# A fourth feature block of the down projection in seven half products, the blocks spread over a pair of output columns, and the second gate's sums spread evenly over the gate and up stage

## The chip, the cores and the metric

The kernel runs on one core of one Trainium2 chip. The metric is the device time of one execution in microseconds (us); lower is better. The core has a matrix engine (TensorE, PE in the profile; its weight loads are PEld), a vector engine (VectorE, DVE), an activation engine (ScalarE, ACT), GpSimd (POOL) and a sync engine (SP), from whose queue nearly all transfers are issued.

## The reference, cut to what matters

The reference is one layer of a diffusion transformer over 256 latent tokens and 256 context tokens, in float32, with a model width of 2048 and a hidden width of 5632. After attention, its output projection and a layer norm comes the part that the change touches:

```python
def swiglu(u, w_gate, w_up, w_down):
    return (jax.nn.silu(u @ w_gate) * (u @ w_up)) @ w_down
...
sh1, sc1, g1, sh2, sc2, g2 = ada_mods(c, w_ada[layer], b_ada[layer])
...
x = layer_norm(DN_ALPHA * x + g2 * swiglu(modulate(x, sh2, sc2), w_gate[layer], w_up[layer], w_down[layer]),
               ln2_g[layer], ln2_b[layer])
```

Here `u` is 256 x 2048, `w_gate` and `w_up` are 2048 x 5632, `w_down` is 5632 x 2048. The vector `g2` is the "second gate": 2048 numbers, each the product of the 2048 entries of `silu(c)` with a column of `w_ada`.

## The kernel before, in words

**Products in three passes.** A float32 product is made of three matmuls. Each operand is split into a rounded part `hi` (a copy on ScalarE) and the rest `lo` (a subtraction on VectorE), and `mm3` (L280 to L283) issues hi x hi, hi x lo and lo x hi into one bank of PSUM. `load_split` loads a piece of weights of 512 x 512 (1024 KB) into one of four `raw` buffers and splits it in two operations per engine, of 128 x 1024 each (`split_raw`, L271 and L272; `split`, L277 and L278, does the same for other operands). There are four pairs of `hi` and `lo` buffers, so the splits can be two plain steps ahead of TensorE.

**Gate and up stage.** The hidden width is cut into 11 blocks of 512. For each block `f` a step `project` multiplies 512 of the 2048 model features with 512 columns of `w_gate` or `w_up`, for both halves of the tokens: 24 matmuls. Some of the first steps of each block were done earlier (their sums lie in `spills`). In the stage shown here, blocks 0 to 2 have 6 steps left, blocks 3 to 9 have 4, block 10 has 8: 54 in all. At a block's end `activate` makes silu(gate) * up on VectorE and ScalarE. Then `flip_steps` transposes the result: `squares` within 32 x 32 squares, `put` through DRAM and `get` back (eight stores and two loads on SP), and `place` splits it into `hTh[f]` and `hTl[f]`. These steps are due a fixed number of `turn()` calls later (`PUT`, `GET`, `PLACE`, `QUARTERS`); each step of the gate, up and down stages makes one call, and a block in half products two. Buffers are shared: `hTh[f]` takes the memory of the spill of block f-1.

**The second gate's sums.** `gate2_steps(i)` gives 14 steps for 1024 columns of the gate: eight that load 1024 KB of `w_ada` each and add them up on VectorE in two operations (`vector_sum`, L400), and six that sum over the partitions with TensorE. They use the same `raw` buffers as the weights. `merge` puts lists of steps together evenly. Before, the first half is merged with blocks 0 to 2 (18 steps), the second with blocks 7 to 10 (20 steps); blocks 3 to 6 run without sums, and at their first steps `residual_base` prepares the residual with rows of the layer norm (tile `lgb`, two loads and four VectorE operations per block).

**Down stage.** The output width is four column blocks of 512, handled as two pairs (`pair(0)`, `pair(2)`). A `plain` step multiplies one feature block by 512 columns, for both halves of the tokens: 24 matmuls, two splits on ScalarE and VectorE each. For the blocks in `QUARTERS` the product of a pair, with both operands in 2 x 2 parts (halves of tokens and of features; halves of features and the two column blocks), is made of seven products in place of eight (Winograd's form of Strassen's method): `by_quarters` issues 7 x 6 = 42 matmuls instead of 48. For it `quarter_sums` makes four sums s1 to s4 of parts of the activations once per block, and splits them; and VectorE makes four combinations of the parts of the weights for each pair, each 128 x 1024, between the seven splits. The banks named a and c gather the first column block for the two halves of the tokens, b and d the second, and p1, p5, p6 and p7 are added in at the end (`combine_parts`). `first_block` and `second_block` apply the gate and add the residual. After the last matmuls comes the second layer norm (`ending`).

The order of work is the program's order, in which the tile framework places each engine's instructions as their inputs and buffers come free; within the last lines (`manual_schedule`) it is as written. The order of the feature blocks is given by hand:

```python
QUARTERS = {8: (9, 13), 9: (10, 11), 10: (9, 9)}
ORDER = (0, 1, 8, 2, 3, 9, 4, 5, 6, 10, 7)
```

Each entry of `QUARTERS` holds the turns after which the block's placement and its sums are due. The first column block of a pair runs through all of `ORDER`, with blocks 8, 9 and 10 in half products for both column blocks at once; then the second column block runs through the eight plain blocks.

## Time and profile before

| | before |
|---|---|
| median of 3 runs | 1134.63 us (1134.55 to 1135.07) |
| the profiled execution | 1133.65 us, its span 1131.9 us |
| mean granted clock of TensorE | 0.995 |
| busy: TensorE, VectorE, ScalarE | 1105.7, 923.0, 588.6 us |
| first matmul of the down stage | at 886.42 us |
| start of the last matmul | at 1118.36 us |

A row of the profile's groups names the line and engine, the operation, output and inputs, shapes, the count, then the busy time and the mean duration of one in ns, and last the idle time of the engine before them with what ended it. A row of the timeline begins with start and duration in us. A row of the waits has what waited, what it waited for, and the total, the number and the longest.

### The profile page before, as it was taken

The numbers are of one execution on the slowest core, as the hardware profiler recorded it, in microseconds if no ns is written. First come the engines' busy times: TensorE is split into PE (matmuls) and PEld (weight loads), VectorE is DVE, ScalarE is ACT, GpSimd is POOL, SyncE is SP. The second block draws the span as 40 slices with busy tenths as digits, with TensorE's granted clock in tenths as the row PEclk, the third lists the DMA queues.
The fourth block names the chain that finished last, engine by engine and source line by source line (L and its number), as shares of the span: only waits on it lengthen the run. The fifth ranks groups of instructions, "written<-read, shape, count | busy, mean of one in ns | idle before, by whom it ended". The sixth has DMA issues, their size and how long they took to land. (4 is left out here: it accounts for less than half of the span.)

```text
span 1131.9 us, 14173 instructions
## 1 busy us (share of the span) xinstructions
PE 1105.7 (98%) x5241; PEld 894.3 (79%) x5241; DVE 923.0 (82%) x1133; ACT 588.6 (52%) x843; POOL 41.5 (4%) x79
## 2 busy tenths in 40 slices
PE   8999999999999999999999999999989999999995
PEld 6766778777888788888888888888778888888884
DVE  3768999999998997877699767879874899678876
ACT  3444584977784365444564544454344565345541
POOL 1000050101200010000000000000000000000000
PEclk9999999999999999999999999999999999999998
DMA  9999999687999789989889877779887576546651
GB/s 293 383 384 397 381 354 362 229 302 224 354 339 384 277 295 347 347 285 350 276 275 336 314 233 254 238 245 317 305 302 260 153 253 223 190 148 228 225 216 74
DMA packets 179241, 321.26 MB, mean 284 GB/s; under 512 B 8762, under 2 KB 51162, under 8 KB 176867
## 3 DMA queue, kind: packets, MB, share of 16 engines
q1 hardware_dynamic: 177364, 319.25, 81.2%
q10 hardware_dynamic: 1808, 1.11, 0.4%
q8 instruction: 41, 0.67, 0.2%
q14 instruction: 28, 0.23, 0.1%
HBM read 304.07 MB, written 16.25 MB: 283 GB/s over the span
## 5 line engine op out<-in xcount | busy, mean ns | idle before, releaser
L272 DVE TENSOR_TENSOR lo<-raw,hi 128x1024 fp32r<-128x1024 f32 x234 | 282.0, 1220 | 115.2 <-ACT hi L271 107.5
L271 ACT CAST hi<-raw 128x1024 fp32r<-128x1024 f32 x234 | 244.7, 1054 | 239.9 <-PE acc L283 206.5
L282 PE MATMUL acc<-lo,u2h 128*128 128x512 f32 x704 | 275.2, 391 | 3.1 <-DVE lo L272 3.1
L281 PE MATMUL acc<-hi,u2h 128*128 128x512 f32 x704 | 274.2, 391 | 2.4 <-ACT hi L271 2.4
L283 PE MATMUL acc<-hi,u2l 128*128 128x512 f32 x704 | 275.0, 391 | 1.2 <-DVE u2l L1630 1.2
L282 PEld LDWEIGHTS acc<-lo,u2h 128*128 128x128 f32 x704 | 132.5, 188 | 31.9 <-DVE lo L272 4.6
L281 PEld LDWEIGHTS acc<-hi,u2h 128*128 128x128 f32 x704 | 132.5, 188 | 31.1 <-ACT hi L271 2.8
L283 PEld LDWEIGHTS acc<-hi,u2l 128*128 128x128 f32 x704 | 132.5, 188 | 29.7 <-DVE u2l L1630 2.1
L549 ACT CAST hi<-raw 128x1024 fp32r<-128x1024 f32 (+1 forms) x86 | 87.7, 1033 | 97.5 <-PE acc L283 47.4
L552 DVE TENSOR_TENSOR lo<-raw,hi 128x1024 fp32r<-128x1024 f32 (+1 forms) x86 | 101.4, 1196 | 20.7 <-ACT hi L549 20.4
L400 DVE SCALAR_TENSOR_TENSOR adav<-raw,cs,adav 128x1024 f32<-128x1024 f32 (+1 forms) x96 | 114.4, 1191 | 2.7 <-DMA raw<-in_w_ada_dram 1.7
L281 PE MATMUL acc<-hi,hTh 128*128 128x512 f32 x272 | 105.8, 389 | 0.3 <-ACT hi L277 0.3
L282 PE MATMUL acc<-lo,hTh 128*128 128x512 f32 x272 | 105.8, 389 | 0.0
L283 PE MATMUL acc<-hi,hTl 128*128 128x512 f32 x272 | 105.6, 389 | 0.0
L281 PE MATMUL acc<-hi,uh 128*128 128x512 f32 x256 | 103.4, 404 | 1.3 <-ACT qacc L833 1.3
L282 PE MATMUL acc<-lo,uh 128*128 128x512 f32 x256 | 100.2, 391 | 0.2 <-DVE lo L552 0.2
L283 PE MATMUL acc<-hi,ul 128*128 128x512 f32 x256 | 100.1, 391 | 0.1
L281 PEld LDWEIGHTS acc<-hi,uh 128*128 128x128 f32 x256 | 48.1, 188 | 18.3 <-issue 4.6
L281 PEld LDWEIGHTS acc<-hi,hTh 128*128 128x128 f32 x272 | 51.0, 188 | 11.3 <-ACT hi L277 0.7
L282 PEld LDWEIGHTS acc<-lo,hTh 128*128 128x128 f32 x272 | 51.0, 188 | 10.9 <-DVE lo L272 0.4
L283 PEld LDWEIGHTS acc<-hi,hTl 128*128 128x128 f32 x272 | 51.1, 188 | 10.7
L283 PEld LDWEIGHTS acc<-hi,ul 128*128 128x128 f32 x256 | 48.1, 188 | 10.8 <-DVE ul L784 0.4
(271 smaller groups left out, 1452.3 us busy)
## 6 DMA issues: line engine op xcount, KB each, us to landing
raw<-in_w_ada_dram SPq DMA_DIRECT2D x63, 1024.0 KB, 6.9
raw<-in_w_gate_dram SPq DMA_DIRECT2D x44, 1024.0 KB, 5.4
raw<-in_w_up_dram SPq DMA_DIRECT2D x44, 1024.0 KB, 7.1
raw<-in_w_down_dram SPq DMA_DIRECT2D x44, 1024.0 KB, 5.6
raw<-in_w_ada_dram SPq DMA_DIRECT2D x66, 512.0 KB, 6.4
raw<-in_w_in_dram SPq DMA_DIRECT2D x18, 1024.0 KB, 8.1
raw<-in_w_out_dram SPq DMA_DIRECT2D x16, 1024.0 KB, 7.9
pd<-hx SPq DMA_DIRECT2D x64, 128.0 KB, 3.5
```

The source lines that it names most:

```text
L271: nc.scalar.copy(hi[:, :n], raw[:, s : s + n])
L272: nc.vector.tensor_tensor(lo[:, :n], raw[:, s : s + n], hi[:, :n].bitcast(F32), op=ALU.subtract)
L281: nc.tensor.matmul(ps, lhsT=xh, rhs=w[0], start=first, stop=False, skip_group_check=seeded)
L282: nc.tensor.matmul(ps, lhsT=xh, rhs=w[1], start=False, stop=False, skip_group_check=seeded)
L283: nc.tensor.matmul(ps, lhsT=xl, rhs=w[0], start=False, stop=last, skip_group_check=seeded)
L400: nc.vector.scalar_tensor_tensor(a[:, c : c + piece], raw[:, f : f + piece], cs[:, 4 * (g * (G4 * NB // w) + j) + 2, None], a[:, c : c + p ...
L549: nc.scalar.copy(hl.hi[:, :n], raw.t[:, s : s + n])
L552: nc.vector.tensor_tensor(hl.lo[:, :n], raw.t[:, s : s + n], hl.hi[:, :n].bitcast(F32), op=ALU.subtract)
```

## The change

It makes feature block 7 a fourth block in half products. The blocks' order is written out for each pair with steps of both column blocks: a is a plain step of the first, b of the second, s a block in half products for both. The s blocks now come after two or three plain steps each, the last one after the first steps of the second column block. In `by_quarters` the product s4 x b22 comes first, and the combinations of the weights overwrite the loaded parts, three of them in a row behind p1's split; before they used a tile of their own. `quarter_sums` makes and splits its four sums in two halves through a small tile `qs`, and all four blocks' split sums lie in the memory that the gate and up stage's input used. The layer-norm rows of `residual_base` go to two of the four small tiles `t2k` instead of `lgb`. The 28 steps of the second gate are merged evenly with all 54 steps of the gate and up stage. Near the end, `l2_loads` (the second layer norm's rows) is issued after the last weights, and the last three feature blocks are 4, 5 and 6.

```diff
-QUARTERS = {8: (9, 13), 9: (10, 11), 10: (9, 9)}
-ORDER = (0, 1, 8, 2, 3, 9, 4, 5, 6, 10, 7)
+QUARTERS = {7: (9, 17), 8: (15, 15), 9: (14, 14), 10: (10, 10)}
+ORDERS = ('a0 a1 a2 s7 a3 a4 s8 a5 a6 s9 b0 b1 b2 s10 b3 b4 b5 b6', 'a0 a1 a2 s7 a3 a4 s8 a5 a6 s9 b0 b1 s10 b2 b3 b4 b5 b6')
...
     def residual_base(n):
-        lgb = pb.tile([P, 2, NB], F32, tag="lgb", name="lgb")
-        lg, lb = lgb[:, 0, :], lgb[:, 1, :]
+        lg, lb = t2k("lg"), t2k("lb")
...
     def quarter_sums(f, hf):
...
-            room["q"] = [both[:, 0], both[:, 1], pb.tile([P, 2, 4, 2, P], F32R, tag="u2l0", name="quarters")]
-            room["x"] = pb.tile([P, 2, 2 * NB], F32, tag="u2l1", name="sums")
-        quarters[f] = [room["q"][i][:, c] for c in range(2)]
-        sums = room["x"][:, 0].rearrange("p (s q t) -> p s q t", s=4, q=2)
...
-        for o, x0, x1, op in ((s1, a21, a22, ALU.add), (s2, s1, a11, ALU.subtract), (s3, a11, a21, ALU.subtract),
-                              (s4, a12, s2, ALU.subtract)):
-            nc.vector.tensor_tensor(o, x0, x1, op=op)
-        split(*quarters[f], sums)
+            room["q"] = [both[:, 0], both[:, 1]]
+            room["q"] += [pb.tile([P, 2, 4, 2, P], F32R, tag=f"u2l{j}", name="quarters") for j in range(2)]
+        hi, lo = quarters[f] = [room["q"][i][:, c] for c in range(2)]
+        pair = pb.tile([P, 2, 2, P], F32, tag="qs", name="sums")
+        one, two = (pair[:, c].rearrange("p q (a i) -> p q a i", a=4) for c in range(2))
...
+        nc.vector.tensor_tensor(one, a21, a22, op=ALU.add)
+        nc.vector.tensor_tensor(two, one, a11, op=ALU.subtract)
+        split(hi[:, 0:2], lo[:, 0:2], pair)
+        nc.vector.tensor_tensor(one, a11, a21, op=ALU.subtract)
+        nc.vector.tensor_tensor(two, a12, two, op=ALU.subtract)
+        split(hi[:, 2:4], lo[:, 2:4], pair)
...
-    run(merge(sum((ffn[f] for f in range(BASE_F)), []), gate2_steps(0)))
-    run(sum((ffn[f] for f in range(BASE_F, BASE_F + 4)), []))
-    run(merge(sum((ffn[f] for f in range(BASE_F + 4, FFN // NB)), []), gate2_steps(1)))
+    run(merge(sum(ffn.values(), []), gate2_steps(0) + gate2_steps(1)))
...
     def by_quarters(f, n, bank, begins, ends):
...
-            ("p1", "a11", b11, (x1, b22, b12, sub)),
-            ("b", "s4", b22, (b12, b12, b11, sub)),
-            ("a", "a12", b21, (x2, x1, b11, add)),
-            ("p7", "s3", x1, (b21, b21, x2, sub)),
+            ("b", "s4", b22, None),
+            ("p1", "a11", b11, ((b22, b22, b12, sub), (b12, b12, b11, sub), (b11, b22, b11, add))),
+            ("a", "a12", b21, None),
+            ("p7", "s3", b22, ((b21, b21, b11, sub),)),
             ("p5", "s1", b12, None),
-            ("p6", "s2", x2, None),
+            ("p6", "s2", b11, None),
             ("c", "a22", b21, None),
...
-    one = pair(0)
-    run(one[0])
-    second_start(0, 1, one[5])
-    one[2]()
-    run(one[1][1:3])
-    one[3]()
-    run(one[1][3:])
-    two = pair(2)
-    run(two[0][:2])
-    one[4]()
-    run(two[0][2:])
-    second_start(0, 3, two[5])
-    two[2]()
-    l2_loads()
-    run(two[1][1:3])
-    two[3]()
-    run(two[1][3:-3])
-    ws = [load_split(w_down, f * 4, 3 * NB, spare=i == 2) for i, f in enumerate(two[6][-3:])]
+    parts, combine_parts, first_block, second_block, _ = pair(0)
+    head, mid, tail, rest = parts("b3", "b4", "b5")
+    run(head + mid)
+    combine_parts()
+    run(tail)
+    first_block()
+    run(rest)
+    parts, combine_parts, first_block, last_block, bank = pair(2)
+    head, mid, tail, rest, end = parts("a2", "b2", "b3", "b4")
+    run(head)
+    second_block()
+    run(mid + tail)
+    combine_parts()
+    run(rest)
+    first_block()
+    ws = [load_split(w_down, f * 4, 3 * NB, spare=f == 6) for f in (4, 5, 6)]
+    l2_loads()
```

More of the change, by code (lines that the diff above doesn't have):

```diff
@@ L1737, in mms @@
             mm3(ps, hTh[f][:, j, tt], hTl[f][:, j, tt], w[j], first and j == 0, last and j == 3)
-    def plain(f, n, accs, begins, ends):
-        w = load_split(w_down, f * 4, n * NB)
-        for t in range(NT):
-            mms(f, w, t, accs[t], begins, ends)
-        turn()
     def by_quarters(f, n, bank, begins, ends):
@@ L1747, in by_quarters @@
         (b11, b12), (b21, b22) = ([r[:, :, :NB], r[:, :, NB:]] for r in (r1, r2))
-        x1, x2 = (room["x"][:, i].rearrange("p (k n) -> p k n", k=2) for i in range(2))
         h = [(c[f][:, 0:2, :P], c[f][:, 2:4, :P], c[f][:, 2:4, P:]) for c in (hTh, hTl)]
@@ L1764, in by_quarters @@
             split(hi, lo, right)
-            if after:
-                nc.vector.tensor_tensor(after[0], after[1], after[2], op=after[3])
-            own = len(name) == 2
+            for o, x0, x1, op in after or ():
+                nc.vector.tensor_tensor(o, x0, x1, op=op)
+            own = name != "b"
             for j in range(2):
@@ L1785, in begins, with step, plain_step @@
             return fresh
-        whole = [f for f in ORDER if f not in QUARTERS]
-        parts = [f for f in ORDER if f in QUARTERS]
-        def first(f):
-            if f in QUARTERS:
-                return lambda: by_quarters(f, n, bank, begins, f == parts[-1])
-            return lambda: plain(f, n, (bank("a"), bank("c")), begins("a") | begins("c"), f == whole[-1])
-        def second(f):
-            return lambda: plain(f, n + 1, (bank("b"), bank("d")), False, f == whole[-1])
+        order = ORDERS[n // 2].split()
+        last = {k: [o for o in order if o[0] == k][-1] for k in "abs"}
+        steps = {}
+        def step(kind, f):
+            if kind == "s":
+                return lambda: by_quarters(f, n, bank, begins, f"s{f}" == last["s"])
+            ps, col = ("ac", n) if kind == "a" else ("bd", n + 1)
+            def plain_step():
+                w = load_split(w_down, f * 4, col * NB)
+                for t in range(NT):
+                    mms(f, w, t, bank(ps[t]), begins(ps[t]), f"{kind}{f}" == last[kind] and kind == "b")
+                turn()
+            return plain_step
+        for o in order:
+            steps[o] = step(o[0], int(o[1:]))
         def combine_parts():
```

17 lines of the change are left out of this document (7 added, 10 removed).

## The prediction

> **What bounds the kernel now.** I read the page's head first, then the table by stretches, then TensorE's waits, and last VectorE's order of work in the two stages that the change touches.
>
> ```profile
> span 1131.9 us, 14173 instructions
> PE 1105.7 (98%) x5241; PEld 894.3 (79%) x5241; DVE 923.0 (82%) x1133; ACT 588.6 (52%) x843; POOL 41.5 (4%) x79
> ```
>
> TensorE is busy for 98% of the span. So time can be won in two ways: fewer matmuls, or fewer of the 26 us in which it does not run. Busy time is no price for a matmul, because matmuls overlap. The start times are; these are the first two and the last matmul of the down projection, and below them its groups:
>
> ```profile
> 886.42 0.39 PE L281 MATMUL acc<-hi,hTh 128*128 128x512 f32 x1
> 886.65 0.39 PE L282 MATMUL acc<-lo,hTh 128*128 128x512 f32 x1
> ...
> 1118.36 0.39 PE L283 MATMUL acc<-hilo,hTl 128*128 128x512 f32 x1
> L281 PE MATMUL acc<-hi,hTh 128*128 128x512 f32 x272 | 105.8, 389 | 0.3 <-ACT hi L277 0.3
> L281 PE MATMUL wk<-hi,quarters 128*128 128x512 f32 x36 | 13.9, 390 | 0.0
> L281 PE MATMUL acc<-hi,quarters 128*128 128x512 f32 x12 | 4.7, 389 | 0.0
> L281 PE MATMUL wk<-hi,hTh 128*128 128x512 f32 x12 | 4.7, 389 | 0.0
> L281 PE MATMUL acc<-hilo,hTh 128*128 128x512 f32 x8 | 3.1, 389 | 0.0
> ```
>
> Each group stands three times (L281, L282, L283), so the stage has 3 x (272+36+12+12+8) = 1020 matmuls. The 1019 steps from 886.42 to 1118.36, less the one wait of 0.3, take 231.6 us: 0.2273 us a matmul, not 0.39. The stage is a gapless row of matmuls. The next table shows where TensorE does lose time; its columns are length, then busy time (and instructions) of each engine, clock, DMA share, GB/s:
>
> ```profile
> 500.00:540.00 40.00, 40.00 (x178) 33.14 (x177) 30.58 (x26) 19.53 (x23) 0.00 (x0) 1.00 0.99 354
> 750.00:797.00 47.00, 47.00 (x209) 38.93 (x208) 42.92 (x47) 20.99 (x24) 0.00 (x0) 1.00 0.88 300
> 797.00:842.00 45.00, 39.51 (x164) 31.17 (x163) 34.50 (x38) 19.45 (x25) 0.00 (x0) 0.96 0.86 289
> 830.00:840.00 10.00, 10.00 (x38) 8.03 (x38) 8.57 (x10) 5.97 (x9) 0.00 (x0) 0.83 0.75 217
> 842.00:886.40 44.40, 44.40 (x197) 36.71 (x196) 25.33 (x27) 18.80 (x20) 0.00 (x0) 1.00 0.73 252
> PE acc L282 <- DVE lo L272: 3.1, 3, 1.5
> PE acc L281 <- ACT hi L271: 2.4, 1, 2.4
> ACT hi L271 <- DMA raw<-in_w_up_dram: 4.2, 1, 4.2
> ```
>
> From 842 to 886 the gate and up stage runs 197 matmuls in 44.4 us, 0.2254 each. At that pace the 45 us from 797 to 842 would hold 199.7, and they hold 164. The 35.7 that are missing are 8.0 us: 5.5 of idle time, and the rest in a slower clock. TensorE waits there for the two halves of split weights, and ScalarE, which starts the split, waited 4.2 us for the weights to land. This is the stretch in which the second gate's column sums share the last blocks.
>
> **The terms, one by one.** *Matmuls.* A plain step is 24 matmuls, a block in seven half products is 7 x 6 = 42 for a pair of column blocks instead of 48. One more such block in both pairs removes 12: 12 x 0.2273 = 2.7 us. Nothing covers TensorE in this stage, so all of it counts: **-2.7**.
>
> *The sums in the gate and up stage.* Before, the second half's 14 steps are spread over the 20 steps from block 7 on: eight loads of 1024 KB, one per 1.43 steps, 0.70 a step. After, 28 steps lie on 54: a load per 1.93 steps, 0.52 a step, and the second half's eight run from late in block 5 to the end of block 8. One step of TensorE is 24 x 0.2267 = 5.44 us (886.65 less 886.42 is 0.23), a block of four is 21.8. The DMA issues and VectorE's rows of a block:
>
> ```profile
> raw<-in_w_up_dram SPq DMA_DIRECT2D x44, 1024.0 KB, 7.1
> hd<-spill SPq DMA_DIRECT2D x80, 64.0 KB, 5.0
> spill<-hd SPq DMA_DIRECT2D x20, 256.0 KB, 5.6
> lgb<-in_ln_g_dram SPq DMA_DIRECT2D x4, 256.0 KB, 5.4
> L400 DVE SCALAR_TENSOR_TENSOR adav<-raw,cs,adav 128x1024 f32<-128x1024 f32 x10 | 12.8, 1279 | 0.0
> L1519 DVE TENSOR_TENSOR spill<-spill,acc 128x512 f32<-128x512 f32 x12 | 7.7, 680 | 0.0
> L1505 DVE SCALAR_TENSOR_TENSOR xt<-xt,lgb 128x512 f32<-128x512 f32 x4 | 2.6, 688 | 0.0
> 782.80 0.69 DVE L278 TENSOR_TENSOR hTl<-spill,hTh 128x512 fp32r<-128x512 f32 x1
> 783.40 1.28 DVE L400 SCALAR_TENSOR_TENSOR adav<-raw,cs,adav 128x1024 f32<-128x1024 f32 x1
> 784.59 1.22 DVE L272 TENSOR_TENSOR lo<-raw,hi 128x1024 fp32r<-128x1024 f32 x1
> 785.73 1.28 DVE L400 SCALAR_TENSOR_TENSOR adav<-raw,cs,adav 128x1024 f32<-128x1024 f32 x1
> ```
>
> From start to start a 512-wide operation takes 0.60 us, a sum 1.19, a split 1.14. So a block costs VectorE 8 splits (9.1), ten 512-wide operations (L1519, L1520, L1523, L1533 and the placement, twice each: 6.0) and the sums. With 0.70 loads a step, two sums each, that is 2.8 x 2 x 1.19 = 6.7, together 21.8 of 21.8 us: no slack at all. With 0.52 it is 4.9, together 20.0; block 6, which also prepares the residual (four operations, 2.4 us), has 22.4, and its 0.6 us are less than the two steps by which the splits run ahead. On the DMA side a block needs 4 + 2.8 loads of 1.05 MB plus 1.05 MB for its spill's way out and back: 8.2 MB, 376 GB/s; after 7.4 MB, 341 GB/s, and some 364 where the layer-norm rows of block 6 come with it. The stretch 500 to 540, with denser sums than the new ones but no spills, moves 354 and loses nothing; 750 to 797, which begins with the second half's first load, moves 300 and uses up its lead until TensorE stalls: a deficit of 46 us x (376 - 300) = 3.5 MB, within the 4 MB of raw buffers. The new order's deficit at 300 GB/s would be 33 us x 60 + 43 us x 41 = 3.7 MB, just at the lead; at 354 it has none. So between none and about 1 us of the stall stays by supply; the bounds are 0 and all 8.0. I take 0.7, nearer to the row at 354, because VectorE's slack returns the buffers sooner: -8.0 + 0.7 = **-7.3**.
>
> The Trainium skill ("DMA: Bandwidth & Descriptors", Where 436 GB/s comes from) puts the HBM's limit for one core at about 358 GB/s. By it the old 376 had to stall, the new order hardly would, and the sum would have 0 in place of my 0.7; the row of 790 to 800 agrees only roughly, since it moved more:
>
> ```profile
> 790.00:800.00 10.00, 10.00 (x45) 8.27 (x45) 7.68 (x10) 3.06 (x3) 0.00 (x0) 1.00 1.04 397
> 828.46 0.73 PE L281 MATMUL acc<-hi,u2h 128*128 128x512 f32 x2 [2.38 <-ACT hi L271]
> 831.10 0.63 PE L281 MATMUL acc<-hi,u2h 128*128 128x512 f32 x1
> 831.53 0.63 PE L282 MATMUL acc<-lo,u2h 128*128 128x512 f32 x1
> ```
>
> After the wait of 2.38 us matmuls start 0.43 apart until 834, some 1.6 us lost: a remaining wait of that size costs its length and 1.6 more. The Trainium skill ("TensorE: Matmul & The Clock Gate", What's actually happening) lets the clock fall only after an idle window of about 3.4 us; by it a stall of 2.4 would cost 2.4 alone, and here the trace is the stricter.
>
> *VectorE in the down stage.* A plain step costs it two splits, 2.3 us against 5.44 of TensorE. A half-product block costs seven splits and four combinations of weights, 11 x 1.14 = 12.5 against 9.5. It must live on its lead of two steps.
>
> ```profile
> 1019.60 1.22 DVE L278 TENSOR_TENSOR lo<-raw,hi 128x1024 fp32r<-128x1024 f32 x1
> 1020.74 5.16 DVE L272 TENSOR_TENSOR lo<-raw,hi 128x1024 fp32r<-128x1024 f32 x4
> 1027.69 1.23 DVE L1766 TENSOR_TENSOR sums<-raw 128x1024 f32<-128x1024 f32 x1 [1.79 <-DMA raw<-in_w_down_dram]
> raw<-in_w_down_dram SPq DMA_DIRECT2D x44, 1024.0 KB, 5.6
> L1568 DVE TENSOR_TENSOR sums<-spill 128x256 f32<-128x256 f32 x4 | 1.6, 417 | 0.0
> L277 ACT CAST hi<-raw 128x1024 fp32r<-128x1024 f32 x30 | 31.5, 1055 | 37.3 <-PE acc L283 32.4 <-PE wk L283 1.7 <-issue 1.4
> ```
>
> In the first pair the activations' work stands in between too: block 10's products and transposes 4 x 0.6 = 2.4, four sets of sums at 2.5 (four operations of about 0.34 apart, one split), three placements at 1.2. At the start one and a half plain steps are split already (3.4). To the end of s7 TensorE has 3 x 5.44 + 9.52 = 25.8 us, VectorE 6.8 - 3.4 + 12.5 + 2.4 + 5.0 + 1.2 = 24.5; to the end of s8 46.2 against 45.2; to the end of s9 66.6 against 65.9. The splits are needed about a product (1.36) early, so each of the three runs some tenths late, together about 1.2 us; before, the same account gave one wait of 0.3. The bounds are -0.3 (none) and 3.0 (12.5 - 9.5) at each of the three, 9; I take the ledger's difference, **+0.9**. The sums are now split in two halves: two 512-wide ones, 1.20 against 1.14, inside that ledger. In the second pair no such work stands between, and nothing is added.
>
> *Edits that I cost at little.* The new order of the seven products issues the same eleven operations; the three combinations in a row after p1 (3.4 us) are covered by b and p1 and by the preceding step. The tile of sums is gone, and layer-norm rows use the shared small tiles; their loads queue on SP behind weights, but the tiles' earlier users are a block older. At the end five plain steps (27.2 us) follow s10 where nine did; the combined blocks' 16 operations (9.6) and ten splits (11.4) still fit, with up to 1.5 us late when the last three steps' splits stand behind them: **+0.3**. The second layer-norm's rows wait for s10's operands and then have 27 us for a load of two tiles. The chain after the last matmul is untouched.
>
> **Sum.** -2.7 - 7.3 + 0.9 + 0.3 = -8.8 against this execution's 1133.65, 1.0 below the median of the runs shown; on the median 1134.63 that is **1125.8**. With all residues gone it is 1134.6 - 2.7 - 8.0 - 0.3 = 1123.6.
>
> **Rivals.** *The stall stays* (chance 0.16). If the lateness at 797 comes from SP's queue, in which eight spill stores stand in a row ahead of the next weights, and not from the density, it returns in blocks 5 to 8. Against it: every earlier block sends the same stores, and none of TensorE's three waits on split weights lies before 797. Time: 1134.6 - 2.7 + 1.2 = 1133.1, no change.
>
> *The raw buffers' hand-over* (0.17). The first product is now the one that needs the half of the weights which the block before gave back last. From c's split (ends 1020.8) to that load's use took 6.9 us; then cast 1.06 and eleven operations 12.5, a loop of 20.4, and TensorE's loop of one such block and two plain steps is 9.5 + 10.9 = 20.4. There is no slack from s to s; before, p1 could start without that half. With 1.5 us more per loop, five loops (two in the first pair, three in the second) less a lead of 1.2 in each pair cost 5.1 us: 1130.9.
>
> *Slower* (0.06): the same place, with the load landing later, since it now queues beside its twin issued only 1.1 us earlier. From a hand-over of 9.5 us on (2.6 more: 5 x 2.6 - 2.4 = 10.6) the gain is gone; at 11 us it costs 5 x 4.1 - 2.4 = 18 and gives 1144. The median landing of 5.6 us speaks against it. Another 0.04 I leave to slower times that I cannot name.
>
> **How the numbers follow.** The forecast has 0.57, 1123.6 to 1129. A change under 0.2%, 2.3 us, can't be told from none. Faster: 0.57, 0.17 and a quarter of the first rival, 0.78; same: 0.12; slower: 0.10. The range reaches from 1123.0 to 1131.8, over the forecast, most of the hand-over and the stall's lighter forms.
>
> **What would show it.** Right: 1008 matmuls in the down stage; no row of TensorE waiting between the start of block 5 and 886, clock 1.00 there; the stage some 7 us earlier at its end; waits of tenths at s7 to s9. Wrong: waits for split weights in blocks 5 to 8; or ScalarE waiting for raw of the down weights ahead of every half-product block, with TensorE idle behind it.

## The result, and the profile after

The changed kernel takes 1145.63 us (median of 4 runs, 1143.91 to 1146.66) against 1134.59 us (4 runs, 1133.27 to 1135.07) for the kernel before on the same chip: a ratio of 1.0097, interval 1.0081 to 1.0112. It is 11 us slower, where 9 us faster was forecast. The page of the changed kernel begins:

```profile
span 1143.4 us, 14187 instructions
PE 1107.7 (97%) x5229; PEld 890.3 (78%) x5229; DVE 940.4 (82%) x1156; ACT 595.1 (52%) x854; POOL 40.5 (4%) x79
```

The 12 matmuls are gone (5241 to 5229), and still the span grew by 11.5 us. Three places account for it. "Lost" is summed over the matmuls' start times: wherever the next start comes more than 0.08 us later than the usual 0.2268 us, the excess counts (from 560 us on).

| | before | after | difference |
|---|---|---|---|
| first matmul of the down stage | 886.42 | 892.03 | +5.6 |
| lost in the gate and up stage until then | 8.2 | 13.4 | |
| first to last matmul of the down stage | 231.9 | 236.0 | +4.1 |
| lost in the down stage | 0.9 | 7.2 | |
| last matmul to the end of the span | 13.5 | 15.35 | +1.8 |

**Gate and up stage.** The table by stretches of the changed kernel (columns as in the prediction), and TensorE's waits from 640 to 890 with one row of ScalarE's:

```profile
713.00:759.00 46.00, 45.41 (x200) 37.19 (x199) 38.77 (x45) 20.29 (x24) 0.00 (x0) 1.00 0.87 291
759.00:830.00 71.00, 62.76 (x257) 48.48 (x258) 55.83 (x64) 29.88 (x38) 0.00 (x0) 0.98 0.82 274
850.00:892.00 42.00, 42.00 (x187) 34.79 (x186) 21.49 (x21) 16.45 (x16) 0.00 (x0) 1.00 0.64 212
PE acc L282 <- DVE lo L272: 5.4, 9, 0.8
PE acc L281 <- ACT hi L271: 3.4, 2, 1.7
ACT spill L1521 <- DVE spill L1518: 27.1, 4, 11.8
```

The stall did not go: it moved from 797 to 842 into 759 to 830, 257 matmuls in 71 us where a gapless row would hold 313. VectorE is busy for only 55.8 of those 71 us and the loads move 274 GB/s, less than the 291 just ahead of them. Neither is full. What happens shows in the timeline around one wait; each bracket holds the idle time before the row and what ended it. Behind it is the last row of the DMA view for 764 to 786, its rate in 40 slices of 0.55 us:

```profile
767.14 7.89 SPq L251 DMA_DIRECT2D raw<-in_w_up_dram  x2
782.04 0.69 DVE L1518 TENSOR_TENSOR spill<-spill,acc 128x512 f32<-128x512 f32 x1 [3.35 <-PE acc L283]
782.76 0.63 ACT L1521 ACTIVATE spill<-spill 128x512 f32<-128x512 f32 x1 [11.76 <-DVE spill L1518]
783.30 1.98 ACT L271 CAST hi<-raw 128x1024 fp32r<-128x1024 f32 x2
784.38 0.73 PE L281 MATMUL acc<-hi,u2h 128*128 128x512 f32 x2 [1.70 <-ACT hi L271]
784.44 4.70 DVE L272 TENSOR_TENSOR lo<-raw,hi 128x1024 fp32r<-128x1024 f32 x4
785.71 0.79 PE L282 MATMUL acc<-lo,u2h 128*128 128x512 f32 x1 [0.60 <-DVE lo L272]
...
GB/s 380 374 342 338 195 100 112 60 223 402 365 424 372 406 410 413 413 242 7 0 0 71 112 302 402 406 417 406 406 413 432 365 432 387 186 22 30 7 86 138
```

ScalarE stood idle for 11.76 us. Its next instruction in order was the silu of a block (L1521), which waits for VectorE's addition of the block's gate sums (L1518), which waits for TensorE's last matmuls of the block's gate half. Behind the silu stood the casts of the block's up weights (L271), and they follow it without a gap. The first of the two loads was issued at 767.1; the DMA engines moved nothing in the slices from 774.5 to 775.5, so it had landed by then, nine microseconds before its cast. TensorE ran out of split weights and waited 1.70 and 0.60 us. This is a queue with a blocked head: the next step's splits stand behind the end of a block's half, and that end waits for TensorE. A raw buffer that is not split comes back late, and the next load starts late too; with that fits that the rate falls to nothing, or nearly, twice in that row.

The framework does not place the silu alike in all blocks. Counted along ScalarE's queue, in blocks 3, 4, 5 and 9 it stands behind four casts of up weights, as many as there are pairs of buffers, in block 6 behind two, and in blocks 7 and 8, where TensorE stalls, behind none.

**Down stage.** TensorE's and ScalarE's waits from 886 on, a load's landing from the page, and the hand-over of which the prediction spoke:

```profile
PE acc L281 <- ACT hi L277: 1.9, 3, 0.6
PE wk L282 <- DVE lo L278: 1.7, 4, 0.5
...
ACT hi L277 <- DVE raw L1758: 13.2, 14, 1.3
ACT hi L277 <- DMA raw<-in_w_down_dram: 12.6, 4, 4.5
...
raw<-in_w_down_dram SPq DMA_DIRECT2D x44, 1024.0 KB, 7.3
...
1030.93 3.49 DVE L278 TENSOR_TENSOR lo<-raw,hi 128x1024 fp32r<-128x1024 f32 x3
1042.18 2.00 ACT L277 CAST hi<-raw 128x1024 fp32r<-128x1024 f32 x2 [4.31 <-DMA raw<-in_w_down_dram]
1043.27 2.36 DVE L278 TENSOR_TENSOR lo<-raw,hi 128x1024 fp32r<-128x1024 f32 x2 [4.13 <-ACT hi L277]
1045.55 3.74 DVE L1758 TENSOR_TENSOR raw<-raw 128x1024 f32<-128x1024 f32 x3
```

The two loads of a block in half products are now issued 1.1 us apart (1033.31 and 1034.44) instead of 2.3, and the median landing of the down weights is 7.3 us instead of 5.6. From the end of c's split (1034.4) to the cast of the new half took 7.8 us, 6.9 in the trace before. And the three combinations of L1758 in a row keep the next split from VectorE for 3.74 us.

**The end.** The last products of the first token half, t0, and of the second, t1; the first row is the start of t1's part in the kernel before, the others are of the changed kernel:

```profile
1119.40 0.68 DVE L1193 TENSOR_TENSOR yt<-acc,adav 128x512 f32<-128x512 f32 x1
1121.67 0.69 DVE L1193 TENSOR_TENSOR yt<-acc,adav 128x512 f32<-128x512 f32 x1 [2.03 <-PE acc L283]
1127.80 2.73 DVE L1716 SCALAR_TENSOR_TENSOR xt<-xt,ly,l 128x512 f32<-128x512 f32 x4
1128.05 0.39 PE L283 MATMUL acc<-hilo,hTl 128*128 128x512 f32 x1
1130.45 0.68 DVE L1193 TENSOR_TENSOR yt<-acc,adav 128x512 f32<-128x512 f32 x1
```

VectorE begins t1's part 2.40 us after the last matmul's start, because it is still busy with t0's (until 1130.5); before it began after 1.04 (1119.40 against 1118.36). The framework had placed six of t1's matmuls ahead of t0's last ones, so t0's chain began later against the end.

### The profile page after: what moved, and what is told of

It reads as the page before. It is cut to its first block, busy times and chain, and to the rows that moved or that the text cites. A ratio compares the mean times of both kernels' runs of the same rounds, so it can differ in the third digit from the quotient of the medians.

```text
span 1143.4 us, 14187 instructions
## 1 busy us (share of the span) xinstructions
PE 1107.7 (97%) x5229; PEld 890.3 (78%) x5229; DVE 940.4 (82%) x1156; ACT 595.1 (52%) x854; POOL 40.5 (4%) x79
## 5 line engine op out<-in xcount | busy, mean ns | idle before, releaser
L271 ACT CAST hi<-raw 128x1024 fp32r<-128x1024 f32 x226 | 236.0, 1054 | 213.7 <-PE acc L283 179.0
L272 DVE TENSOR_TENSOR lo<-raw,hi 128x1024 fp32r<-128x1024 f32 x226 | 271.2, 1220 | 87.6 <-ACT hi L271 86.7
L281 PE MATMUL acc<-hi,hTh 128*128 128x512 f32 x248 | 96.4, 390 | 1.9 <-ACT hi L277 1.9
L282 PE MATMUL acc<-lo,hTh 128*128 128x512 f32 x248 | 96.9, 391 | 0.5 <-DVE lo L272 0.5
L283 PE MATMUL acc<-hi,hTl 128*128 128x512 f32 x248 | 96.5, 389 | 0.0
L277 ACT CAST hi<-raw 128x1024 fp32r<-128x1024 f32 x56 | 58.6, 1053 | 57.5 <-PE acc L283 30.8
L278 DVE TENSOR_TENSOR lo<-raw,hi 128x1024 fp32r<-128x1024 f32 x56 | 66.6, 1219 | 20.3 <-ACT hi L277 20.3
L281 PEld LDWEIGHTS acc<-hi,hTh 128*128 128x128 f32 x248 | 46.5, 188 | 12.8 <-ACT hi L277 3.2
```

What stands on the lines that cost most here:

```text
L271: nc.scalar.copy(hi[:, :n], raw[:, s : s + n])
L272: nc.vector.tensor_tensor(lo[:, :n], raw[:, s : s + n], hi[:, :n].bitcast(F32), op=ALU.subtract)
L277: nc.scalar.copy(hi, src)
L278: nc.vector.tensor_tensor(lo, src, hi.bitcast(F32), op=ALU.subtract)
L281: nc.tensor.matmul(ps, lhsT=xh, rhs=w[0], start=first, stop=False, skip_group_check=seeded)
L282: nc.tensor.matmul(ps, lhsT=xh, rhs=w[1], start=False, stop=False, skip_group_check=seeded)
```

## The experiments

The kernel each diff starts from is named first. A ratio stands to the kernel before on the same chip. "Lost" and the other stage numbers are from one profiled execution each, so some tenths of them are chance.

| run | median us | ratio (interval) | down stage begins | lost before it | first to last matmul | lost there | end |
|---|---|---|---|---|---|---|---|
| before | 1134.59 | | 886.42 | 8.2 | 231.9 | 0.9 | 13.5 |
| after | 1145.63 | 1.0097 (1.0081 to 1.0112) | 892.03 | 13.4 | 236.0 | 7.2 | 15.35 |
| a_oldmerge | 1139.09 | 1.0052 (1.0037 to 1.0067) | 887.09 | 7.4 | 235.1 | 6.4 | 14.9 |
| a_silu | 1142.18 | 1.0077 (1.0061 to 1.0094) | 889.68 | 12.6 | 236.1 | 7.3 | 14.6 |
| a_noload | 1130.99 | 0.9976 (0.9961 to 0.999) | 878.31 | 0.1 | 235.8 | 7.0 | 15.0 |
| a_nosum | 1143.11 | 1.0086 (1.0066 to 1.0106) | 892.17 | 12.8 | 235.3 | 6.6 | 14.8 |
| a_p1first | 1142.32 | 1.0074 (1.0052 to 1.0097) | 891.09 | 13.5 | 232.3 | 3.7 | 15.6 |
| a_tail | 1144.37 | 1.0092 (1.0072 to 1.0112) | 892.50 | 14.6 | 236.8 | 8.1 | 13.8 |
| a_three | 1139.89 | 1.0059 (1.0043 to 1.0075) | 891.55 | 13.4 | 232.8 | 1.7 | 13.5 |
| b_spread | 1137.57 | 1.0025 (1.0014 to 1.0037) | 890.62 | 13.0 | 231.9 | 0.9 | 13.8 |
| a_hand | 1134.37 | 0.9999 (0.9988 to 1.001) | 881.35 | 3.9 | 235.1 | 6.4 | 14.9 |
| a_late | 1143.91 | 1.0077 (1.0057 to 1.0097) | 891.54 | 13.2 | 235.8 | 7.1 | 14.9 |
| b_hand | 1139.77 | 1.0041 (1.0027 to 1.0055) | 893.24 | 14.5 | 231.7 | 0.7 | 13.2 |
| a_p1_nosums | 1138.91 | one run | 892.13 | 13.5 | 229.8 | 1.2 | 15.2 |
| best_a | 1131.58 | 0.9974 (0.9964 to 0.9984) | 883.38 | 5.3 | 234.4 | 5.6 | 13.5 |
| best_a2 | 1133.39 | 0.9986 (0.9975 to 0.9997) | 885.87 | 5.5 | 233.8 | 5.1 | 13.3 |
| best_b | 1131.34 | 0.9966 (0.9953 to 0.9978) | 887.54 | 6.9 | 231.9 | 0.9 | 13.4 |

**1. The old merge in the changed kernel (a_oldmerge).**

```diff
-    run(merge(sum(ffn.values(), []), gate2_steps(0) + gate2_steps(1)))
+    run(merge(sum((ffn[f] for f in range(BASE_F)), []), gate2_steps(0)))
+    run(sum((ffn[f] for f in range(BASE_F, BASE_F + 4)), []))
+    run(merge(sum((ffn[f] for f in range(BASE_F + 4, FFN // NB)), []), gate2_steps(1)))
```

> The changed kernel with one part undone: the second gate's sums merged with blocks 0 to 2 and 7 to 10 as before; the four blocks in half products, their order and the rest stay. Theory: the even spread by itself made the gate and up stage worse (13.3 us lost there against 8.2 before), so undoing it brings the stage back to some 8 us lost, the down stage's first matmul to 886 to 887 and the time to 1140 (1138.5 to 1141.5), still above before by the down stage's waits and the longer end. Rival: the stage got worse by the layer-norm rows in the shared small tiles or by the moved placement, not by the spread; then the loss stays near 13 us and the time near 1145.

The down stage begins 4.9 us earlier, about where it began before (887.09 and 886.42). So the even spread itself, not the fourth block or the moved tiles, costs the gate and up stage some 5 us. The fourth block's cost stays.

**2. Loads or VectorE's time (a_noload, a_nosum).** The second gate's loads go (`held` is set for its steps alone), or most of its arithmetic (`few`):

```diff
 a_noload
-            raw = raw_tile()
-            vector_load(raw, starts, width, g)
+            raw = xt[:, 0, :] if held else raw_tile()
+            if not held:
+                vector_load(raw, starts, width, g)
 a_nosum
-        nc.vector.scalar_tensor_tensor(a[:, c : c + piece], raw[:, f : f + piece],
...
+        n = 64 if few else piece
+        nc.vector.scalar_tensor_tensor(a[:, c : c + n], raw[:, f : f + n],
```

> The changed kernel with the second gate's 16 loads of 1024 KB left out: VectorE's 32 sums read a tile that is there already, so their time on VectorE stays and the transfers and raw buffers are freed (the gate's values are no longer the reference's). Theory, supply by transfers and raw buffers: the gate and up stage loses under 2 us, the time is near 1132 to 1134. Rival, VectorE's time: the sums still cost it 38 us in the stage and the loss stays above 8 us, 1140 or more.

> The changed kernel with the second gate's sums made over 64 of 1024 columns: all 16 loads and their raw buffers stay, VectorE's part falls from 38 us to some 5 (the gate's values are no longer the reference's). Theory, supply by transfers: the loads compete as before and the gate and up stage still loses more than 5 us, 1137 or more; the buffers come back earlier, so somewhat less than 13 us. Rival, VectorE's time: the loss falls under 2 us, 1132 to 1134.

The stretch from 713 to 840 of the changed kernel, then of a_nosum, then of a_noload:

```profile
713.00:840.00 127.00, 118.17 (x501) 93.93 (x501) 101.81 (x115) 55.16 (x67) 0.00 (x0) 0.99 0.84 280
```

```profile
713.00:840.00 127.00, 119.25 (x505) 96.02 (x504) 88.12 (x117) 55.62 (x68) 0.00 (x0) 0.97 0.83 282
```

```profile
713.00:840.00 127.00, 127.00 (x561) 105.02 (x561) 112.25 (x129) 62.28 (x73) 0.00 (x0) 1.00 0.74 242
```

Freeing VectorE of 13.7 of 101.8 us gives 4 matmuls more; without the loads there are 60 more, with VectorE busier than ever (112.25), since it does the same sums and TensorE needs more splits. VectorE's time, one of the two amounts that I had priced, is not the cause. Without the loads the stall is gone, but a_noload does not say by what: it takes away their bytes, their turn in the raw buffers and their place in SP's queue, and the framework places the rest differently too. In its trace the silu stands behind at least four casts of up weights in every block from 3 to 9, and from 640 to 890 ScalarE waits 0.2 us before it for VectorE's additions, against 27.1 in the changed kernel. Which of these counts was not told apart.

**3. Density (b_spread).** The kernel before with the second half of the sums spread over blocks 3 to 10: 14 steps on 36, 0.39 a step, instead of 14 on 20, 0.70. The first half stays in blocks 0 to 2. The layer-norm rows use the small tiles, as in the changed kernel.

```diff
-    run(sum((ffn[f] for f in range(BASE_F, BASE_F + 4)), []))
-    run(merge(sum((ffn[f] for f in range(BASE_F + 4, FFN // NB)), []), gate2_steps(1)))
+    run(merge(sum((ffn[f] for f in range(BASE_F, FFN // NB)), []), gate2_steps(1)))
```

> The kernel before with the second gate's first half on blocks 0 to 2 as it is and its second half spread over blocks 3 to 10 (36 steps, a load per 2.6 steps in place of 1.4; layer-norm rows in the shared small tiles so that the second half can begin). Theory, supply of raw buffers by the loads: a block asks for some 316 GB/s, little over the 300 that the stalled stretches move, so the gate and up stage's loss falls from 8.2 us to below 3 and the time from 1133.8 to 1127 to 1130. Rival: any load of the second gate beside blocks that store spills starts the same stall, whatever the density, and a longer stretch stalls longer (as it did in the changed kernel); then the loss is 8 us or more and the time 1133 to 1139.

Fewer loads per step stall more: 13.0 us lost against 8.2, as the rival had it. So in the placed order the stall does not follow the density. One row of the waits and the timeline of it show the same queue with a blocked head, this time VectorE's:

```profile
PE acc L282 <- DVE lo L272: 7.6, 5, 4.5
...
742.08 1.06 ACT L271 CAST hi<-raw 128x1024 fp32r<-128x1024 f32 x1 [1.41 <-PE acc L283]
744.75 1.05 ACT L271 CAST hi<-raw 128x1024 fp32r<-128x1024 f32 x1 [1.61 <-PE acc L283]
746.79 1.36 DVE L1519 TENSOR_TENSOR spill<-spill,acc 128x512 f32<-128x512 f32 x2 [1.84 <-PE acc L283]
750.50 0.65 DVE L1505 SCALAR_TENSOR_TENSOR xt<-lb,xt 128x512 f32<-128x512 f32 x1
752.34 0.79 PE L282 MATMUL acc<-lo,u2h 128*128 128x512 f32 x1 [4.45 <-DVE lo L272]
750.00:760.00 10.00, 7.67 (x22) 6.09 (x23) 8.17 (x8) 1.05 (x1) 0.00 (x0) 0.66 0.55 193
```

`hi` of the next weights was ready from 743 and 746 on. VectorE did sums, residual rows, waited 1.84 us for the block's end, did its additions, products and transposes, and only at 751 began the subtraction that TensorE needed. The wait of 4.45 us is followed by a slow clock (0.66 over 10 us).

**4. Products later in the program (a_silu), and the order held (a_hand, a_late, b_hand).** a_silu issues the products and silu two turns later in the program and leaves the placement to the framework. a_hand also puts off the additions, the second gate's sums, the residual rows and the placement of most blocks by two or three turns, each as an entry of `flips`, and holds VectorE's and ScalarE's order as written from block 3 to the second step of block 10. a_late is the same program without holding the order. b_hand does all of a_hand to the kernel before.

```diff
 a_silu
+        steps = [[2, products_of]] + steps
 a_hand
+        steps = [[2, products]] if f < SPLIT_F else []
...
+                    flips.append([3, residual_base(f - BASE_F)])
...
+                flips.append([2, gates])
...
+                                later=lambda f: flips.append([2, f]))
...
+    with tc.manual_schedule(engines={ET.DVE, ET.Activation}):
+        run(steps[at[0] : at[1]])
 a_late
-    with tc.manual_schedule(engines={ET.DVE, ET.Activation}):
```

> The changed kernel with ScalarE's silu (and the products and transposes behind it) of blocks 0 to 9 put two turns later in the program; nothing is added or left out. Theory of the order: in the stalled stretch ScalarE stands for 11.8 us at a block's silu, which waits for VectorE's addition of the last gate sums, and the casts of the next weights stand behind it although their loads have landed; with silu behind those casts most of the 13.3 us lost in the gate and up stage go: below 5 us lost, time 1135 to 1139. Rival, supply: the weights come too late because the loads, VectorE's sums and the four raw buffers are at their limit; then the order of silu hardly matters and the loss stays above 10 us, time 1143 to 1146.

> The changed kernel with the order of VectorE and ScalarE written out by hand from block 3 to block 10's second step: the additions of a finished gate or up sum, silu, products, transposes, residual rows and the second gate's sums stand behind the splits of the next two steps; loads, operations, buffers and bytes are the same. Theory of the order: the stall in the gate and up stage is VectorE and ScalarE standing at a block's end for TensorE with the next weights' splits queued behind; with them in front, the 13.4 us lost there fall below 3 and the time to 1133 to 1137. Rival, supply: the weights themselves arrive too late beside the second gate's loads; then the loss stays above 8 us and the time above 1140.

> The same program as the one with the order by hand, but placed by the framework as it is in the changed kernel. Theory of the order: the framework places by its own estimate of when the loads land, so the later place in the program alone moves little: 8 to 13 us lost, 1139 to 1145. Rival: the later place in the program is enough; then under 3 us lost.

> The kernel before (three blocks in half products, the second gate's sums on blocks 0 to 2 and 7 to 10) with the same order by hand. Theory of the order: its 8.2 us lost in the gate and up stage fall below 3, the time from 1133.8 to 1126 to 1129, faster than both kernels. Rival, supply: with eight loads in the 11 steps of blocks 7 to 9 the loss stays above 5 us, 1131 or more.

a_silu missed its forecast (12.6 us lost) and told nothing of the mechanism: in its trace ScalarE still stands before the silu, because the framework placed it where it was before:

```profile
ACT spill L1524 <- DVE spill L1518: 29.7, 5, 9.9
```

a_hand and a_late issue the same operations and loads. The waits of ScalarE in a_hand from 640 to 880, its stretch, and the stretch of a_late:

```profile
ACT hi L271 <- DMA raw<-in_w_up_dram: 22.9, 6, 6.5
ACT hi L271 <- DMA raw<-in_w_gate_dram: 22.2, 7, 7.4
...
713.00:840.00 127.00, 124.93 (x544) 101.26 (x544) 115.15 (x130) 59.73 (x72) 0.00 (x0) 1.00 0.90 307
```

```profile
713.00:840.00 127.00, 118.55 (x503) 95.79 (x502) 102.25 (x115) 56.21 (x68) 0.00 (x0) 0.97 0.81 277
```

Held: 544 matmuls, 3.9 us lost, 1134.37 us. Placed: 503, 13.2 lost, 1143.91 us. ScalarE's row "spill from DVE spill" is gone; ScalarE now arrives first and waits for the weights themselves, 45 us in 13 waits. The loads move 307 instead of 277 GB/s, which fits buffers that come back sooner. SP issues its transfers in the same order in both, but for four layer-norm rows, which come later in a_hand, and three gate loads, which a_hand has behind a spill store and a_late ahead of it. So the order on VectorE and ScalarE is the cause of the changed kernel's stall: with it alone the stall comes and goes. b_hand is a miss. With 0.70 loads a step it loses 14.5 us, more than the kernel before, and its waits are again for weights on their way:

```profile
ACT hi L271 <- DMA raw<-in_w_gate_dram: 24.7, 7, 6.3
```

So with the order held, density does matter: 0.70 loads a step are too many for that order, with 0.52 only 3.9 us are lost. Why the placed order did better than the held one at 0.70 (8.2 lost) I did not find out, so how much of the old kernel's 8.2 the order makes stays open.

**5. The down stage (a_p1first, a_three, a_p1_nosums) and the end (a_tail).**

```diff
 a_p1first
-            ("b", "s4", b22, None),
-            ("p1", "a11", b11, ((b22, b22, b12, sub), (b12, b12, b11, sub), (b11, b22, b11, add))),
-            ("a", "a12", b21, None),
+            ("p1", "a11", b11, None),
+            ("b", "s4", b22, ((b22, b22, b12, sub), (b12, b12, b11, sub))),
+            ("a", "a12", b21, ((b11, b22, b11, add),)),
 a_three
-QUARTERS = {7: (9, 17), 8: (15, 15), 9: (14, 14), 10: (10, 10)}
...
+QUARTERS = {8: (9, 13), 9: (10, 11), 10: (9, 9)}
+ORDERS = ('a0 a1 s8 a2 a3 s9 a4 a5 a6 a7 s10 b0 b1 b2 b3 b4 b5 b6 b7',) * 2
...
 a_p1_nosums (a_p1first, and)
-        nc.vector.tensor_tensor(one, a21, a22, op=ALU.add)
...
+            nc.scalar.copy(hi[:, c].rearrange("p q (a i) -> p q a i", a=4), part)
 a_tail
+    with tc.manual_schedule(engines={ET.PE}):
         for t in range(NT):
             for f, w in zip((4, 5, 6), ws):
```

> The changed kernel with another order inside a block in half products: p1 first (it needs the raw buffer that comes back first), then b with two of the combinations behind it, a with the third, p7 with the fourth; the same operations otherwise. Theory, hand-over of raw buffers and three combinations in a row: the waits of 0.4 to 0.8 us at each block in half products go, the down stage's 7.2 us lost fall below 3.5, 4 us off the time. Rival, VectorE's whole time in a block in half products (12.5 us against 9.5): the order does not matter, the loss stays at 6 to 7.5 us.

> The changed kernel with three blocks in half products again (8, 9 and 10, at nearly the places that they had before; block 7 plain), but with the new inner order, the new sums and the even spread of the second gate. Theory: the down stage's losses come from the new inner order and hand-over; with two to four plain steps between, the loss is still 3 to 5 us against 0.9 before. Rival: they come from the fourth block's density and four sets of sums; then the loss is 1 to 1.5 us and the down stage is some 3.5 us shorter than the changed kernel's 236, at 232 to 233.

> The changed kernel with p1 first and the four sums of activations left out: ScalarE writes the eight parts instead, VectorE does nothing for them (the output is no longer the reference's). Theory, VectorE's time in the first pair: it was 10 us of sums there; the first pair's 2.9 us lost fall below 1. Rival, the chain of VectorE's combinations and ScalarE's casts inside a block: the loss stays above 2 us.

> The changed kernel with TensorE's order of the last 72 matmuls held as written: the first half of the tokens through blocks 4, 5 and 6, then the second. Theory: the end grew by 1.8 us (15.4 us after the last matmul's start against 13.5) because six matmuls of the second half were put ahead of the first half's last ones, so that its layer norm on VectorE starts only 30 matmuls before the end instead of 36; with the order held the end is 13.5 to 13.9 us again, and the time some 1.5 us less, or as much as the wait for the third block's splits gives back. Rival: the end is longer because VectorE is late with the splits and sums before it; then it stays above 15 us.

ScalarE's waits for the combinations from 886 on, in a_p1first and in a_three, and VectorE in the first pair, 930 to 960, in the changed kernel, in a_p1first and in a_p1_nosums:

```profile
ACT hi L277 <- DVE raw L1758: 7.3, 11, 1.2
```

```profile
ACT hi L277 <- DVE raw L1758: 3.8, 4, 1.2
```

```profile
930.00:960.00 30.00, 28.36 (x120) 21.76 (x119) 28.67 (x30) 17.31 (x18) 0.00 (x0) 1.00 0.39 141
```

```profile
930.00:960.00 30.00, 29.59 (x128) 23.57 (x127) 29.52 (x30) 18.98 (x20) 0.00 (x0) 1.00 0.42 146
```

```profile
930.00:960.00 30.00, 30.00 (x134) 24.68 (x133) 26.89 (x24) 19.02 (x19) 0.00 (x0) 1.00 0.47 169
```

With p1 first and the combinations apart, 3.5 of 7.2 us go, a little less than forecast; the waits at the second pair's blocks vanish, and 2.8 us of the rest lie in the first pair. ScalarE's row of waits for down weights (L277, 12.6 us in the changed kernel) is gone, although the two loads are still issued 1.1 us apart and land after 7.2 us in the median. In the first pair VectorE is busy for 29.5 of 30 us. Without the four sets of sums (24 operations in that stretch in place of 30) it has slack, and the loss is 1.2 us. With three blocks, in the new inner order, it is 1.7 us, 0.8 more than before. So the loss is VectorE's load in the first pair plus the inner order, and that order costs much only beside the fourth block.

a_tail shortens the end by 1.5 us to 13.8 and gives most of it back at once: from 1110 us on TensorE loses 2.0 us, against 0.7 in the changed kernel, because in the held order it waits for splits that the placed order covered. With another 1.2 us lost in the gate and up stage of that one execution, its gain in the median is within its interval.

**6. What the experiments add up to (best_a, best_b, best_a2).** best_a is a_hand with p1first and tail. best_b is b_spread with a_hand's order. best_a2 is best_a with b_spread's spread.

```diff
 best_b (kernel before)
+    steps = merge(sum((ffn[f] for f in range(BASE_F)), []), gate2_steps(0)) + merge(sum((ffn[f] for f in range(BASE_F, FFN // NB)), []), gate2_steps(1))
```

> The changed kernel with three edits that were run singly: VectorE's and ScalarE's order by hand in the gate and up stage, p1 first in the blocks in half products, and TensorE's order of the last matmuls held. If the three act in different places and add up, from 1134.4 with the hand order alone some 3 us in the down stage and 1 at the end go: 1129.5 to 1131.5, with 4 us lost in the gate and up stage. Rival: the end's order gives back at the third block's splits what it wins, and it stays at 1131.5 to 1133.

> The kernel before (three blocks in half products) with the order by hand and the second gate's second half spread over blocks 3 to 10, 0.39 loads a step. Theory, density once the order is held: 14.5 us lost at 0.70 loads a step, 3.9 at 0.52, so under 2 at 0.39; time 1126 to 1128.5. Rival, loads beside spills stall by themselves: 4 us or more lost as in the even spread, 1130 or more.

> As best_a, but with the second gate's second half spread over blocks 3 to 10 as in best_b. Density: the gate and up stage loses under 2 us instead of 4, 1127.5 to 1129.5. Rival: no change against best_a. It also prices the fourth block: against best_b a shorter row of matmuls by 2.7 us, and whatever more is lost in the down stage (some 3 us by the order of products alone), so best_a2 is not faster than best_b.

best_a (1131.58 us) and best_b (1131.34 us) are both faster than the kernel before, by 0.26% and 0.34%. They can't be told from each other, so the fourth block wins nothing here even with the order held. The three edits of best_a do not add up: its down stage still loses 5.6 us where a_p1first lost 3.7, and 1.8 of them fall in the last matmuls, where the held order gives back what the end wins, as the rival said. In best_b the order does what density alone could not: b_spread was 1.0025, best_b is 0.9966, with the same loads. But its gate and up stage lost 6.9 us where under 2 were forecast; the rival had 4 or more. Its profiled execution was the slowest of its seven (1134.73 us): the first of the stage's 54 x 24 matmuls starts at 586.3 us, 4.0 later than in the kernel before, and the begin of the down stage in the table is late by that. Its waits from 640 to 890, and best_a's:

```profile
PE acc L282 <- DVE lo L272: 2.8, 2, 2.6
```

```profile
PE acc L282 <- DVE lo L272: 2.8, 5, 1.4
PE acc L281 <- ACT hi L271: 0.2, 1, 0.2
```

A wait of 2.6 us at 748 stays in best_b and, of the same size, in best_a2; with the slower matmuls behind it it makes some 4.5 of best_b's 6.9 us. Two rows of best_b's timeline show how it arises:

```profile
739.87 2.01 ACT L271 CAST hi<-raw 128x1024 fp32r<-128x1024 f32 x2
747.36 2.35 DVE L272 TENSOR_TENSOR lo<-raw,hi 128x1024 fp32r<-128x1024 f32 x2
```

The casts were done at 741.9, but VectorE first placed a block, did four residual rows and two sums of the second gate, without a gap, and came to the subtractions 5.5 us later. So the order by hand has a head of its own, busy instead of blocked, where sums and rows fall due together. A lighter spread than 0.52 brought best_a2 nothing over best_a: 5.5 us lost instead of 5.3, and again not the under 2 that was forecast.

## Why the prediction was wrong, step by step

**Matmuls, -2.7: right in kind, a little too large.** 12 fewer on the page. From the first to the last matmul of the down stage, less what is lost there, it is 236.0 - 7.2 = 228.8 us against 231.9 - 0.9 = 231.0, and 228.6 in a_p1_nosums: 2.2 to 2.4 less.

**The sums in the gate and up stage, -7.3: the step that failed.** It measured +5.6 at the stage's end. I read the stall as a matter of amounts (loads per step, VectorE's time per block, GB/s) because the sums were dense where it lay. But VectorE's time does next to nothing (a_nosum 12.8), and in the placed order fewer loads per step stall more (b_spread 13.0). What decides in the changed kernel is which instruction stands at the head of ScalarE's and VectorE's queues when TensorE comes to the end of a block's gate or up half; held by hand, the same loads lose 3.9 instead of 13.4. The loads take part in it: without them the stall is gone (0.1 lost), and with the order held too many of them still stall (b_hand 14.5).

The wrong reading began in the trace before. I put TensorE's waits down to ScalarE waiting 4.2 us "for the weights to land". That wait ended at 795.5 us. The longest of TensorE's waits, 2.38 us at 828.46, had another cause, and these rows of the kernel before show it:

```profile
ACT spill L1522 <- DVE spill L1519: 14.4, 2, 10.8
813.73 0.39 SPq L251 DMA_DIRECT2D raw<-in_w_up_dram  x1
826.17 1.31 ACT L1522 ACTIVATE spill<-spill 128x512 f32<-128x512 f32 x2 [10.75 <-DVE spill L1519]
827.38 1.98 ACT L271 CAST hi<-raw 128x1024 fp32r<-128x1024 f32 x2
```

The load of the up weights was issued at 813.73 and landed after 5.2 us; ScalarE stood for 10.75 us before the silu and cast them only at 827.38. The blocked head was there already, and my price of 8.0 us for a lack of supply rested on not seeing it.

"The stall stays" had 0.16, with SP's queue of spill stores as its mechanism. The stall did stay, and grew; but a_hand sends the same stores and is nearly free of it, so that mechanism is not what made it.

**VectorE in the down stage, +0.9, and the last steps, +0.3: mis-sized, together they measured +6.3.** s7, s8 and s9 lost 1.1, 1.2 and 1.6 in the first pair, where I had some tenths each; the second pair, where I added nothing, lost 0.6 to 0.8 at three of its four blocks; and the last steps lost 0.7. The ledger was right that the first pair is full (28.7 of 30 us) but counted work as if it could be done in any order. The inner order, which I had costed at nothing, was worth 3.5. It has two parts, which a_p1first undid together: the product that comes first needs the half of the weights that is loaded last, and three combinations stand in a row. The rival "hand-over" named the first of them: at 1042.18 ScalarE waits for that load, 7.8 us behind c's split instead of 6.9. It priced the two pairs at 5.1 us together. At the next block, at 1063.54, ScalarE waits last for TensorE and not for a load, so the hand-over is not the whole of it.

**"The chain after the last matmul is untouched": wrong, +1.8.** Its instructions are, but VectorE reached it late, because the placed order of TensorE's last matmuls changed. a_tail took 1.5 us of it back and lost 1.3 us ahead of the last matmul for it.

**The clock.** The waits of 1.70 and 0.60 us at 784 are followed by matmuls 0.43 us apart until about 789, as the prediction read it before; from 786 to 789 the granted clock was 0.53. The same two waits at 812 are not: from 809 to 819 it was 1.00. So the length of a wait alone does not say whether the clock falls. After the 4.45 us of b_spread it was 0.66 over 10 us. The Trainium skill ("TensorE: Matmul & The Clock Gate", What's actually happening) lets the clock fall only after an idle window of about 3.4 us; at 784 the trace is again the stricter.

**The limit of 358 GB/s** that the Trainium skill gives for one core ("DMA: Bandwidth & Descriptors", Where 436 GB/s comes from) did not bind: the changed kernel moves 274 GB/s over its stall, and 400 and more in single slices of the DMA row above.

## What to carry to other kernels

Before pricing a stall by amounts, look at what stands at the head of the queues of the engines that feed the bound: an idle engine whose next instruction waits for the bound engine itself, with the next step's inputs already landed, is an order problem, and spreading work more evenly can make it worse. Look at the length of that idle time before an engine's wait for a load is taken for the cause. Where a framework places the instructions, changing the program's order may not change the placed one; a kernel with the order held, beside the same program without, tells the two apart in one run. A ledger of busy time that comes out full says that every operation's place now matters; its difference is then too small a price (here some 1.2 us for three blocks that lost 3.9).

## What was not expected of the hardware

- The median landing of a down-weight load of 1024 KB is 7.3 us where the two loads of a block are issued 1.1 us apart, and 5.6 in the kernel before, where they are issued 2.3 apart.
- On VectorE four splits of 1.22 us each take 4.70 us as a row: they start 1.16 apart. The three combinations, of which the second and third overwrite a part that the one before read, start 1.25 apart and take 3.74.
- What a wait costs behind its end: in b_spread's stretch 750 to 760 stand 22 matmuls where 44 fit, 5.0 us missing. 2.3 us of it are the wait's part in the stretch (750.0 to 752.34), and the other 2.7 the slower pace after it.
